# The first block's way out computed transposed, and its window attention by pairs of heads

## The chip, the cores and the metric

One NeuronCore of one Trainium2 chip runs the program. The metric is the device time of one execution in microseconds (us); lower is better. The core's engines work through their own instruction queues: PE (TensorE, matrix products), DVE (VectorE), ACT (ScalarE), POOL (GpSimd) and SP (SyncE, which issues the DMAs).

## The reference

A first block turns `x` (256 tokens, width 1024) into a new `x`; two layers of a second block follow. What the change touches, cut down:

```python
# first block
o_na = window_attention(q, k, v, kc, vc, rpb)        # 8 heads of 64; per head 256 queries
#   s  = concat([q k_band^T + bias (masked by column), q kc^T])   # 256 x 512 per head
#   pr = softmax(s);  o = pr[:, :256] v + pr[:, 256:] vc
o_dn = bidirectional_delta_rule(...)                  # chunks of 64, 8 heads
u_na = (o_na * silu(z_na)) @ w_o_na
u_dn = (rmsnorm(o_dn) * silu(z_dn)) @ w_o_dn
y    = sigmoid(g_na) * u_na + sigmoid(g_dn) * u_dn
x    = x + gate * (y @ w_out)                         # gate: a third of silu(c) @ mod_w + mod_b
# second block, i = 0, 1
x = layer_norm(ALPHA * x + 0.5 * swiglu(x, ffn1_up[i], ffn1_down[i]))
...
ple = sigmoid(x @ w_ple_gate[i]) * (p[i] @ w_ple[i])
...
```

## The kernel before, in words

All weights stream once from HBM. `block` loads a block of up to 128x1024 (`raw<-W`, issued by SP, line 108), ACT rounds it to the high part `wh` (line 119), and DVE or POOL subtracts for the low part `wl` (line 122); the letters of `self.low` choose which of the two. `mm3` (lines 146 to 150) then makes three products, high by high, high by low and low by high. `raw` has three buffers and `wh` and `wl` four each. Products of data that is not split are plain fp32; the trace shows two records for each of those.

The order of instructions on every engine is fixed when the program is built, by a scheduler that simulates a timeline: it starts from program order and pulls later work forward where an engine would be idle and the buffers are there. So the projections `z_na`, `z_dn`, `g_na` and part of `o_na` are traced after the attention, and run between its instructions.

In the first block the order of the code is: modulation and projections; a loop over 8 heads that builds the two triangular matrices of the delta rule (lines 621 to 645); `invert_blocks` (lines 650 to 682), 31 steps of two multiplications and two subtractions on DVE, each on the result of the step before; `attend` for 8 heads (lines 415 to 446); `levels32` and `levels64` on PE, which need the inverse; the steps of the state; the gates, `o_na`, `g_dn` and `o_dn`; the projection `out` (lines 952 to 958).

`attend(h)` works on 2 tiles of 128 queries by 512 keys. Even heads use the PSUM banks of `nab` (two), odd ones those of `st` (four, shared with the loop over the triangular matrices). Per tile: scores on PE (L433: 64 rows of the array, even heads the first 64 and odd heads the last 64), bias and maximum on DVE (L435, L436), exponential with the sum on ACT (L437), reciprocal on DVE (L438), a scaling of all 512 columns on ACT (L439), four transpositions on PE into one bank and a copy on ACT (`rows_T`, L373 and L376), and then eight products with the values (L445), whose output is on partitions 0 to 63 for even heads and 64 to 127 for odd ones. The bias tile (two buffers) is loaded by two DMAs (L422), masked on POOL (L423), and last read by L435.

The way out: `out` is computed with the tokens on the partitions, in four PSUM banks, 512 columns wide: first output columns 0 to 511 for k = 0 to 7, then 512 to 1023. `mod_gate` has made `gate` as rows on all partitions (L902, L904). Two DVE operations for each quarter (L966, L967) make `x1`. `second` then builds the rope tables (L1025 to L1049, on DVE with two sines on ACT), transposes `x1` on PE (16 times, L1068) and splits the result (L153, L154), makes the projection `ple(0)` (24 products of 512 columns), multiplies `x1` by ALPHA on POOL (L999), and starts the feed-forward network `ffn` (L1155): for each f of 22 two `up` products of 24 matmuls of 256 columns, and `down` products.

Of the kernel before, what the change touches and what calls it, by code (L numbers as in the profile page):

```python
# [92 lines left out]
class Kernel:  # L93
# [84 lines left out]
    def run(self):  # L178
        nc = self.nc
        with self.st:  # L180
            one = self.one = self.pool("one")
            self.st_p = self.pool("st", 4, space=PSUM)


            self.cols = one.tile([128, 192], FP32, name="cols")[:, 0:NCOLS]
            self.ident = one.tile([128, 128], FP32, name="ident")
            self.mhalf = self.pool("edge", side="right").tile([128, 24], FP32, name="mhalf")[:, 0:1]
            nc.vector.memset(self.mhalf, -0.5)
            with ExitStack() as s1:
                x1 = self.first(s1)  # L190
                if self.upto == "first":
                    nc.sync.dma_start(out=self.out.rearrange("(t p) d -> p t d", p=128), in_=x1)
                    return
            with ExitStack() as s2:
                self.second(s2, x1)
# [6 lines left out]
    def first(self, st):  # L202
# [15 lines left out]
        P4, PR, MR, S1, X8 = tag("P4", 1024, 1, early), tag("PR", 256, 2, early), tag("MR", 512, 1), tag("S1", 512, 2, early), tag("X8", 2048, 1, self.one)  # L218
# [26 lines left out]
        sel4 = one.tile([4, 2], FP32, name="sel4")  # L245
        nc.vector.tensor_tensor(out=sel4, in0=self.ident[0:4, 0:2], in1=self.ident[0:4, 2:4], op=ALU.add)

        sel3 = one.tile([4, 1], FP32, name="sel3")
        nc.vector.tensor_tensor(out=sel3, in0=sel4[:, 0:1], in1=self.ident[0:4, 1:2], op=ALU.add)
# [70 lines left out]
        identR = one.tile([128, 128], F32R, name="identR")  # L320
# [8 lines left out]
        ones = one.tile([128, 16], FP32, name="ones")[:, 0:1]  # L329
        nc.vector.memset(ones, 1.0)  # L330
        ab = one.tile([128, 32], FP32, name="ab")
# [4 lines left out]
        xT[0] = tuple(one.tile([128, 8, 256], F32R, name=n) for n in ("xh", "xl"))  # L336
# [78 lines left out]
        def attend(h, ways=0):  # L415

            e, j = h % 2, h // 2
            sl = slice(64 * e, 64 * e + 64)
            bank, P = (nab, F2) if ways == 0 else (self.bank, U2)
            bias = one.tile([128, 6, 64], FP32, tag="bias", bufs=2, name="bias")  # L420
            for r2 in range(2):
                nc.sync.dma_start(out=bias[64 * r2:64 * r2 + 64], in_=I["rpb"][:, h, 1 - r2:7 - r2, :])  # L422
            nc.gpsimd.tensor_tensor(out=bias, in0=bias, in1=cc["namask"].unsqueeze(1).to_broadcast([128, 6, 64]), op=ALU.add)  # L423
            if ways == 0:
                pt = P4().rearrange("p (t c q) -> p t c q", t=2, c=4)
                pt = [pt[:, 0], pt[:, 1]]
            else:
                pt = [Y2().rearrange("p (c q) -> p c q", c=4) for _ in range(2)]
            ps, pr = [bank() for _ in range(2)], [P() for _ in range(2)]
            mx = one.tile([128, 4], FP32, tag="smmx", bufs=4, name="mx")  # L430
            mx, rs = mx[:, 0:2], mx[:, 2:4]
            for t in range(2):
                nc.tensor.matmul(out=ps[t], lhsT=nqT[sl, j, t * 128:(t + 1) * 128], rhs=nkT[sl, j, :], start=True, stop=True)  # L433
            for t in range(2):
                nc.vector.tensor_tensor(out=ps[t][:, 0:256], in0=ps[t][:, 0:256], in1=bias[:, 2 - 2 * t:6 - 2 * t, :].rearrange("p e c -> p (e c)"), op=ALU.add)  # L435
                nc.vector.tensor_reduce(out=mx[:, t:t + 1], in_=ps[t], axis=AX.X, op=ALU.max, negate=True)  # L436
                nc.scalar.activation(out=pr[t], in_=ps[t], func=ACT.Exp, bias=mx[:, t:t + 1], accum_out=rs[:, t:t + 1])  # L437
                nc.vector.reciprocal(out=rs[:, t:t + 1], in_=rs[:, t:t + 1])  # L438
                nc.scalar.mul(out=pr[t], in_=pr[t], mul=rs[:, t:t + 1])  # L439
            for t in range(2):  # L440
                rows_T(pr[t], pt[t], 0, bank=bank)
            po = bank()
            for t in range(2):
                for c in range(4):
                    nc.tensor.matmul(out=po[sl, t * 128:(t + 1) * 128], lhsT=nv[:, c, h * 64:(h + 1) * 64], rhs=pt[t][:, c, :], start=(c == 0), stop=(c == 3))  # L445
            nc.scalar.copy(out=oT[sl, j, :], in_=po[sl, 0:256])
# [367 lines left out]
        for h in range(8):  # L814
            attend(h, h % 2)
# [75 lines left out]
        gate = None  # L891

        def mod_gate(c):

            nonlocal gate
# [56 lines left out]
        ps = [[acc() for _ in range(2)], [nab() for _ in range(2)]]  # L952
        for c in range(2):
            for k in range(8):
                w = self.block(("out", k), c, 2)
                for t in range(2):
# [786 lines left out]
```

## Time and profile before

| | us |
|---|---|
| median of 3 runs | 1791.49 |
| lowest, highest | 1790.18, 1792.56 |
| the profiled execution | 1789.8 |
| span of its profile | 1787.9 |
| PE busy in it | 1701.7 |

Times in the rows are in us from the start of the span. A row of the timeline or of the chain has a start and a duration. `PE` is the matrix product and `PEld` the load of its stationary operand, which overlaps it. "x8" means that eight like instructions in a row are merged; in the timeline, the duration of such a row includes the tail of the last one, and in the chain it does not. Matmuls are pipelined, so what one costs is the distance between the starts of two neighbours, which is shorter than its own duration. A bracket at the end of a row is the idle time of that engine before it and what ended it. PEclk is the granted clock of TensorE as a share of full speed: 1.00 is 2.4 GHz, 0.50 is 1.2 GHz.

### The profile page before, as it was taken

To read this page: it belongs to the slowest core of one execution; us is meant where nothing else is said; L and a number is where in the kernel's file an instruction comes from. 1 tells how busy PE (TensorE), PEld (TensorE's weight loads), DVE (VectorE), ACT (ScalarE), POOL (GpSimd) and SP (SyncE) were. 2 spreads that over 40 slices of the span, in tenths; PEclk is the share of its full clock that TensorE was granted. 3 is DMA by queue.
4 is the path that set the end of the run, shared out by engine and by line. 5 is a ranking of instruction groups with operands and counts; after the bars stand their busy time and mean duration, and the time that the engine had idled before them with its cause. 6 is when DMAs were issued, how large, how long until landed. Compare 5 with 4: busy or idle time off the path is not lost.

```text
span 1787.9 us, 30317 instructions
## 1 busy us (share of the span) xinstructions
PE 1701.7 (95%) x12186; PEld 1527.8 (85%) x12186; DVE 1108.0 (62%) x1657; ACT 852.7 (48%) x1372; POOL 350.2 (20%) x235
## 2 busy tenths in 40 slices
PE   6899989999979999999989999899999999989998
PEld 2898866899869998889978999799997899879997
DVE  6774388645665556774676555755568646675556
ACT  6444575433444444653445444444445534444442
POOL 6335342312130002210231000300005103130000
PEclk9899998779989999999999999899999999999999
DMA  7223221312456565544556656565664445645563
GB/s 287 78 83 112 76 67 54 99 41 96 160 199 197 189 201 171 196 149 152 194 166 190 191 191 206 156 205 189 197 204 161 143 164 180 201 162 191 191 208 108
DMA packets 91827, 286.17 MB, mean 160 GB/s; under 512 B 10916, under 2 KB 13476, under 8 KB 91688
## 3 DMA queue, kind: packets, MB, share of 16 engines
q1 hardware_dynamic: 91400, 284.10, 49.1%
q8 instruction: 95, 1.56, 0.4%
q14 instruction: 44, 0.36, 0.1%
q10 hardware_dynamic: 288, 0.16, 0.0%
HBM read 283.17 MB, written 1.05 MB: 159 GB/s over the span
## 4 chain that ended last, share of the span: by engine, by line
PE 79%; DVE 9%; DMA 3%; issue 3%; ACT 2%; POOL 1%; SPq 0%; DVEq 0%; ACTq 0%; POOLq 0%
PE acc L148 13%; PE acc L149 13%; PE acc L150 13%; PE ps L149 10%; PE ps L148 10%; PE ps L150 10%; DMA raw<-W 3%; DVE wl L122 2%; ACT wh L119 1%; PE ps L795 1%; PE ps L725 1%; PE ps L373 1%; DVE PR L671 1%; PE ps L751 1%; PE ps L743 1%
## 5 line engine op out<-in xcount | busy, mean ns | idle before, releaser
L122 DVE TENSOR_TENSOR wl<-raw,wh 128x1024 fp32r<-128x1024 f32 (+1 forms) x462 | 551.0, 1196 | 424.2 <-ACT wh L119 420.9
L119 ACT CAST wh<-raw 128x1024 fp32r<-128x1024 f32 (+1 forms) x535 | 497.8, 934 | 620.8 <-PE acc L149 159.0
L148 PE MATMUL ps<-XH,wh 128*128 128x256 f32 x1408 | 394.9, 281 | 7.1 <-DVE XH L1114 6.7
L149 PE MATMUL ps<-XL,wh 128*128 128x256 f32 x1408 | 395.1, 281 | 5.7 <-DVE XL L154 5.7
L150 PE MATMUL ps<-XH,wl 128*128 128x256 f32 x1408 | 394.0, 280 | 0.0
L148 PEld LDWEIGHTS ps<-XH,wh 128*128 128x128 f32 x1408 | 267.4, 190 | 11.1 <-DVE XH L1114 6.9
L149 PEld LDWEIGHTS ps<-XL,wh 128*128 128x128 f32 x1408 | 266.7, 189 | 9.8 <-DVE XL L154 6.2
L150 PEld LDWEIGHTS ps<-XH,wl 128*128 128x128 f32 x1408 | 268.5, 191 | 0.0
L175 POOL TENSOR_TENSOR rs<-rs,mhalf 128x1 f32<-128x1 f32 x16 | 10.6, 667 | 848.0 <-DVE rs L170 848.0
L122 POOL TENSOR_TENSOR wl<-raw,wh 128x512 fp32r<-128x512 f32 (+1 forms) x73 | 111.1, 1525 | 239.8 <-ACT wh L119 212.2
L148 PE MATMUL acc<-XH,wh 128*128 128x256 f32 x544 | 156.1, 287 | 0.0
L149 PE MATMUL acc<-XL,wh 128*128 128x256 f32 x544 | 153.8, 283 | 0.0
L150 PE MATMUL acc<-XH,wl 128*128 128x256 f32 x544 | 153.7, 283 | 0.0
L148 PEld LDWEIGHTS acc<-XH,wh 128*128 128x128 f32 x544 | 104.7, 192 | 2.0 <-issue 1.0
L150 PEld LDWEIGHTS acc<-XH,wl 128*128 128x128 f32 x544 | 105.1, 193 | 0.0
L149 PEld LDWEIGHTS acc<-XL,wh 128*128 128x128 f32 x544 | 104.4, 192 | 0.0
L148 PE MATMUL acc<-xh,wh 128*128 128x256 f32 (+1 forms) x296 | 88.4, 300 | 8.8 <-ACT wh L119 5.0
L148 PE MATMUL acc<-wh,XH 128*128 128x512 f32 (+1 forms) x216 | 80.0, 405 | 15.5 <-DVE XH L1114 15.2
L150 PE MATMUL acc<-xh,wl 128*128 128x256 f32 (+1 forms) x296 | 88.5, 299 | 3.9 <-DVE wl L122 2.4
L149 PE MATMUL acc<-wl,XH 128*128 128x512 f32 (+1 forms) x216 | 86.8, 403 | 2.6 <-DVE wl L122 2.6
L150 PE MATMUL acc<-wh,H 128*128 128x512 f32 x224 | 88.3, 394 | 0.0
L148 PE MATMUL acc<-wh,H 128*128 128x512 f32 x224 | 88.1, 393 | 0.0
(599 smaller groups left out, 3414.9 us busy)
## 6 DMA issues: line engine op xcount, KB each, us to landing
raw<-W SPq DMA_DIRECT2D x420, 512.0 KB, 4.2
raw<-W SPq DMA_DIRECT2D x145, 256.0 KB, 2.9
GB<-lngb SPq DMA_DIRECT2D x12, 512.0 KB, 5.1
L<-W SPq DMA_DIRECT2D x5, 512.0 KB, 7.4
bias<-rpb SPq DMA_DIRECT2D x16, 96.0 KB, 2.5
M<-c SPq DMA_DIRECT2D x2, 768.0 KB, 4.6
GB<-c SPq DMA_DIRECT2D x2, 768.0 KB, 4.7
A<-x SPq DMA_DIRECT2D x1, 1024.0 KB, 11.1
```

The source lines that it names most:

```text
L119: self.nc.scalar.copy(out=h, in_=raw)
L122: e.tensor_tensor(out=lo, in0=raw, in1=h, op=ALU.subtract)
L148: mm(out=out, lhsT=a[0], rhs=b[0], start=first, stop=False)
L149: mm(out=out, lhsT=a[0], rhs=b[1], start=False, stop=False)
L150: mm(out=out, lhsT=a[1], rhs=b[0], start=False, stop=last)
L175: nc.gpsimd.tensor_tensor(out=out, in0=out, in1=e.to_broadcast(shape), op=ALU.pow)
L373: nc.tensor.transpose(ps[:, j * 128:(j + 1) * 128], src[:, j * 128:(j + 1) * 128], self.ident)
L671: nc.vector.tensor_tensor(out=pr[d], in0=Ln[d][:, j + 1:32, j:j + 1].to_broadcast(sh), in1=X[d][:, j:j + 1, 0:j + 1].to_broadcast(sh), op= ...
L725: nc.tensor.matmul(out=p2[quad[a], m, :], lhsT=tt[quad[b], m, :], rhs=Yd[quad[b], h * 4 + t, :], start=True, stop=True, tile_position=(32 ...
L743: nc.tensor.matmul(out=p1[sb, m, :], lhsT=LTs[d][sa, h, t, sb], rhs=X64[sa, h * 4 + t, :], start=True, stop=True)
L751: nc.tensor.matmul(out=p2[sa, m, :], lhsT=tt[sb, m, :], rhs=LTs[d][sb, h, t, sb], start=True, stop=True)
L795: nc.tensor.matmul(out=pv[:, c], lhsT=LT[:, h, t, :], rhs=r[:, c], start=True, stop=True)
```

## The change

Way out. `out` is computed transposed: the weight block is the stationary operand (blocks are now columns of `w_out`), the output has its 128 output columns on the partitions and 256 tokens across, m = 0 to 7, 24 matmuls of 256 columns each. One DVE operation adds the transposed `x` times the gate, now a column per partition, and a split writes straight into the feed-forward network's input. The 16 transpositions and the four pairs of DVE operations on rows are gone. The rows of `x` times ALPHA, which the first norm needs, are made in `ffn` after f = 4 by 32 products with the identity and four scalings on ACT; the rope tables come after f = 7, and the `ple` projection of layer 0 after f = 10. `mod_gate` transposes its row with eight products of 2 columns, and adds the bias from a constant already there, in place of a DMA and one product of 512 columns.

Attention. `attend(j)` takes heads 2j and 2j+1 together: the score products and the value products of the two alternate. The scaling of the probabilities is gone; the identity is scaled by the reciprocals instead (128 columns, written into the bias tile), and the transposition is a plain product with it. Both heads' values go into one `st` bank, with one copy out.

```diff
+            self.XHa, self.XLa, self.X8 = (tag(n) for n in ("XHa", "XLa", "X8"))
+            self.xt0 = self.new_xt(0)
...
-        def attend(h, ways=0):
...
+        def attend(j):
+            heads = []
+            for e in range(2):
+                h = 2 * j + e
+                bank, P = (nab, F2) if e == 0 else (self.bank, U2)
+                bias = one.tile([128, 6, 64], FP32, tag="bias", bufs=2, name="bias")
...
             for t in range(2):
+                for e, (h, bank, bias, pt, ps, pr, mx, rs) in enumerate(heads):
+                    sl = slice(64 * e, 64 * e + 64)
+                    nc.tensor.matmul(out=ps[t], lhsT=nqT[sl, j, t * 128:(t + 1) * 128], rhs=nkT[sl, j, :], start=True, stop=True)
             for t in range(2):
-                nc.vector.reciprocal(out=rs[:, t:t + 1], in_=rs[:, t:t + 1])
-                nc.scalar.mul(out=pr[t], in_=pr[t], mul=rs[:, t:t + 1])
-            for t in range(2):
-                rows_T(pr[t], pt[t], 0, bank=bank)
-            po = bank()
+                for h, bank, bias, pt, ps, pr, mx, rs in heads:
...
+            for h, bank, bias, pt, ps, pr, mx, rs in heads:
+                nc.vector.reciprocal(out=rs, in_=rs)
+                dg = bias.rearrange("p e c -> p (e c)")
+                for t in range(2):
+                    nc.scalar.mul(out=dg[:, t * 128:(t + 1) * 128], in_=self.ident, mul=rs[:, t:t + 1])
+                for t in range(2):
+                    pp = bank()
+                    for c in range(4):
+                        nc.tensor.matmul(out=pp[:, c * 128:(c + 1) * 128], lhsT=pr[t][:, c * 128:(c + 1) * 128], rhs=dg[:, t * 128:(t + 1) * 128],
+                                         start=True, stop=True)
+                    nc.scalar.copy(out=pt[t], in_=pp.rearrange("p (c q) -> p c q", c=4))
+            po = self.bank()
             for t in range(2):
                 for c in range(4):
+                    for e, (h, bank, bias, pt, ps, pr, mx, rs) in enumerate(heads):
+                        nc.tensor.matmul(out=po[64 * e:64 * e + 64, t * 128:(t + 1) * 128], lhsT=nv[:, c, h * 64:(h + 1) * 64], rhs=pt[t][:, c, :],
+                                         start=(c == 0), stop=(c == 3))
+            nc.scalar.copy(out=oT[:, j, :], in_=po[:, 0:256])
...
         def mod_gate(c):
...
-            nc.sync.dma_start(out=r[1:2, :], in_=I["mod_bg"][:, c * 512:(c + 1) * 512])
             ps = nab()
-            nc.tensor.matmul(out=ps, lhsT=sel3.to_broadcast([4, 128]), rhs=r, start=True, stop=True)
-            gate = gate if c else N4()
-            nc.scalar.mul(out=gate[:, c * 512:(c + 1) * 512], in_=ps, mul=0.5)
+            for q in range(4):
+                nc.tensor.matmul(out=ps[:, 2 * q:2 * q + 2], lhsT=r[:, q * 128:(q + 1) * 128], rhs=sel4, start=True, stop=True)
+            g = gcol[:, c * 4:c * 4 + 4]
...
-        ps = [[acc() for _ in range(2)], [nab() for _ in range(2)]]
-        for c in range(2):
...
+        x0 = Q8().rearrange("p (k t) -> p k t", k=8)
+        nc.sync.dma_start(out=x0, in_=I["xT"])
+        xt = self.new_xt(0)
+        for m in range(8):
+            w = self.blockv(("out", m), "p (k c) -> p k c", k=8)
+            ps = (acc if m % 2 else nab)()[:, 0:256]
             for k in range(8):
+                self.mm3(ps, (w[0][:, k, :], w[1][:, k, :]), (yh[:, k, :], yl[:, k, :]), k == 0, k == 7)
+            v = T2()[:, 0:256]
+            nc.vector.scalar_tensor_tensor(out=v, in0=ps, scalar=gcol[:, m:m + 1], in1=x0[:, m, :], op0=ALU.mult, op1=ALU.add)
+            self.split(xt[0][:, m, :], xt[1][:, m, :], v)
+        return xt
...
-        self.rope_tables()
-        xt = self.transposed(x1)
+        xa = self.X8().rearrange("p (t d) -> p t d", t=2)
+        def first_rows():
+            for t in range(2):
+                for c in range(2):
+                    ps = self.bank()
+                    for k in range(4):
+                        for a in range(2):
+                            nc.tensor.matmul(out=ps[:, k * 128:(k + 1) * 128], lhsT=xt[a][:, 4 * c + k, t * 128:(t + 1) * 128], rhs=self.identR, start=a == 0, stop=a == 1)
+                    nc.scalar.mul(out=xa[:, t, c * 512:(c + 1) * 512], in_=ps, mul=ALPHA)
...
-        nc.gpsimd.tensor_scalar(out=xa, in0=xa, scalar1=ALPHA, scalar2=None, op0=ALU.mult)
         for i in range(2):
-            xt = self.norm(self.ffn(1, i, xt), 0.5, xa, i, 0)
+            xt = self.norm(self.ffn(1, i, xt, {4: first_rows, 7: self.rope_tables, 10: first_ple} if i == 0 else {}), 0.5, xa, i, 0)
...
-    for k in range(8):
-        put(("out", k), inp["w_out"][0][k * 128:(k + 1) * 128])
+    for m in range(8):
+        put(("out", m), kpc(inp["w_out"][0][:, m * 128:(m + 1) * 128], 8))
```

`first_ple` calls `ple_rows`, which makes the same 24 products as `ple` in `st` banks, two at a time. In the second block `XH` and `XL` have one buffer each beside `XHa` and `XLa`, in place of two each.

## Rows read from the trace of the kernel before

**Rows 1.** The page, busy time of the engines over the span.
```profile
PE 1701.7 (95%) x12186; PEld 1527.8 (85%) x12186; DVE 1108.0 (62%) x1657; ACT 852.7 (48%) x1372; POOL 350.2 (20%) x235
```
**Rows 2.** Stretches of 20 us: PE, PEld, DVE, ACT, POOL busy (x); PEclk, DMA, GB/s.
```profile
500.00:520.00 20.00, 9.77 (x41) 8.07 (x40) 17.15 (x24) 8.19 (x12) 15.56 (x5) 0.68 0.53 175
540.00:560.00 20.00, 20.00 (x142) 18.58 (x141) 10.26 (x13) 9.27 (x14) 0.00 (x0) 1.00 0.62 193
```
**Rows 3.** Timeline, 495 to 522: PE, DVE and POOL at the way out.
```profile
495.20 1.03 PE L1068 MATMUL ps<-ident,X 128*128 128x128 f32 x8
...
500.89 0.40 PE L150 MATMUL nab<-wh,B 128*128 128x512 f32 x1
502.07 3.88 DVE L967 TENSOR_TENSOR X<-X,L 128x512 f32<-128x512 f32 x2
503.24 0.66 PE L1068 MATMUL ps<-ident,X 128*128 128x128 f32 x4 [1.96 <-DVE X L967]
506.00 1.11 PE L1068 MATMUL ps<-ident,X 128*128 128x128 f32 x4 [2.10 <-DVE X L967]
508.13 5.37 POOL L999 TENSOR_SCALAR X<-X 128x2048 f32<-128x2048 f32 x1
509.25 4.28 DVE L1031 CAST pf<-pos 128x2 f32<-128x2 int32 x1 [0.71 <-DMA pos<-pos]
510.52 0.41 PE L148 MATMUL ps<-XH,wh 128*128 128x256 f32 x1
515.94 0.68 DVE L154 TENSOR_TENSOR XL<-ps,XH 128x512 fp32r<-128x512 f32 x1
516.67 0.58 PE L149 MATMUL ps<-XL,wh 128*128 128x256 f32 x1 [5.74 <-DVE XL L154]
...
521.20 0.40 PE L148 MATMUL acc<-wh,M 128*128 128x512 f32 x1
```
**Rows 4.** Timeline, two neighbouring matmuls of 256 columns at full clock.
```profile
238.02 0.28 PE L150 MATMUL acc<-xh,wl 128*128 128x256 f32 x1
238.14 0.29 PE L148 MATMUL acc<-xh,wh 128*128 128x256 f32 x1
```
**Rows 5.** Pieces of the chain that ended last: start, us, what, records.
```profile
31.31 1.05 PE ps L303 x8
...
188.56 0.87 PE ps L373 x8
...
197.71 1.91 PE nab L433 x4
...
213.14 1.02 PE nab L445 x8
...
412.26 0.89 PE ps L789 x8
...
419.45 1.05 PE nab L902 x2
...
794.46 1.01 PE ps L1482 x8
```
**Rows 6.** Timeline of PE: value products of an even (nab) and an odd head alternating.
```profile
297.62 0.27 PE L445 MATMUL nab<-P,NV 128*64 128x128 f32 x1
297.67 0.27 PE L445 MATMUL ps<-Y,NV 128*64 128x128 f32 x1
297.73 0.27 PE L445 MATMUL nab<-P,NV 128*64 128x128 f32 x1
```
**Rows 7.** A stretch of 5 us in the attention; columns as in the 20 us stretches.
```profile
270.00:275.00 5.00, 5.00 (x11) 2.13 (x10) 2.41 (x8) 0.80 (x3) 0.99 (x1) 0.50 0.00 0
```
**Rows 8.** Timeline of DVE: the last step of the inversion.
```profile
333.71 1.99 DVE L680 STREAM_TRANSPOSE L<-L 128x1024 f32<-128x1024 f32 x1
```
**Rows 9.** Timeline of SP's queue: DMA issues around the late heads.
```profile
263.98 11.87 SPq L422 DMA_DIRECT2D bias<-rpb  x6
293.58 47.39 SPq L108 DMA_DIRECT2D raw<-W  x22
```

More of the change, by code (lines that the diff above doesn't have):

```diff
@@ L319, in first @@
             cc[n] = c1[:, a:a + C1[n][1]]
-        identR = one.tile([128, 128], F32R, name="identR")
+        identR = self.identR
         nc.vector.tensor_copy(out=identR, in_=self.ident)
@@ L335, in first @@
         xT = {}
-        xT[0] = tuple(one.tile([128, 8, 256], F32R, name=n) for n in ("xh", "xl"))
+        xT[0] = self.xt0
         xc = B16(F32R).rearrange("p (a k t) -> p a k t", a=2, k=8)
@@ L413, in first @@
         oT = one.tile([128, 4, 256], FP32, name="oT")
-        def attend(h, ways=0):
[L417 to L431, printed above, removed]
+        def attend(j):
[4 more added lines that the diff above has]
+                bias = one.tile([128, 6, 64], FP32, tag="bias", bufs=2, name="bias")
+                for r2 in range(2):
+                    nc.sync.dma_start(out=bias[64 * r2:64 * r2 + 64], in_=I["rpb"][:, h, 1 - r2:7 - r2, :])
+                nc.gpsimd.tensor_tensor(out=bias, in0=bias, in1=cc["namask"].unsqueeze(1).to_broadcast([128, 6, 64]), op=ALU.add)
+                if e == 0:
+                    pt = P4().rearrange("p (t c q) -> p t c q", t=2, c=4)
+                    pt = [pt[:, 0], pt[:, 1]]
+                else:
+                    pt = [Y2().rearrange("p (c q) -> p c q", c=4) for _ in range(2)]
+                mx = one.tile([128, 4], FP32, tag="smmx", bufs=4, name="mx")
+                heads.append((h, bank, bias, pt, [bank() for _ in range(2)], [P() for _ in range(2)], mx[:, 0:2], mx[:, 2:4]))
@@ L813, in first @@
         XY = invert_blocks()
-        for h in range(8):
-            attend(h, h % 2)
+        for j in range(4):
+            attend(j)
         def go(*gens):
@@ L1153, in rows_acc, with ffn @@
         return {(t, c): self.acc1() for t in range(2) for c in range(2)}
-    def ffn(self, j, i, xt):
+    def ffn(self, j, i, xt, between={}):
         nc = self.nc
@@ L1187, in ffn @@
                 down(f - 2)
+            if f in between:
+                between[f]()
         down(NF - 2)
@@ L1208, in ple, with ple_rows @@
         yield out
+    def ple_rows(self, i):
+        nc = self.nc
+        p = self.U2().rearrange("p (k t) -> p k t", k=2)
+        nc.sync.dma_start(out=p, in_=self.i["pT"][i])
+        ph = self.M6(F32R)[:, 0:1024].rearrange("p (a k t) -> p a k t", a=2, k=2)
+        self.split(ph[:, 0], ph[:, 1], p)
+        w = [self.block(("ple", i, k)) for k in range(2)]
+        out = self.PL8().rearrange("p (t d) -> p t d", t=2)
+        for t in range(2):
+            acc = {(t, c): self.bank() for c in range(2)}
+            for k in range(2):
+                self.down(acc, w[k], (ph[:, 0, k, :], ph[:, 1, k, :]), k == 0, k == 1, (t,))
+            for c in range(2):
+                nc.scalar.copy(out=out[:, t, c * 512:(c + 1) * 512], in_=acc[t, c])
+        return out
     def ple_gate(self, i, xt, xa, plr):
```

92 lines of the change are left out of this document (32 added, 60 removed).

## The prediction

> **What bounds the kernel now.** I read the page first: PE is busy 95% of the span [rows 1]. So time goes away where PE does not work, works at the low clock, or does work that can be dropped. The table of stretches shows where the first two are. From 540 on PE has no gap at clock 1.00 while the DMAs are 62% busy [rows 2], and the stretches that follow look the same; there a product more or less shows in full. The worst stretch of the whole span is 500 to 520, the way out of the first block: PE 9.77 of 20 us, clock 0.68 [rows 2]. The timeline of that place gives the reasons in order [rows 3]. The last product of `out` starts at 500.89. PE then waits 1.96 and 2.10 us for L967 on DVE, whose two operations take 3.88 us, and starts on `up`. After 510.52 it stands for 5.74 us: the fourth split (L154) sits on DVE behind the rope tables' first cast, L1031, which took 4.28 us for two columns and ended with L999, the multiplication by ALPHA that POOL ran from 508.13 to 513.50. At 521.20 PE is back at its pace.
>
> For the attention I read the chain and the timeline of PE, DVE and SP. Around 270 PE has only the attention: 11 matmul records in 5 us at clock 0.50 [rows 7]. The inversion on DVE ends at 335.7 [rows 8], and `levels32` can't start earlier. Between these two, PE's time is partly spare.
>
> **Way out: what goes.** From 500.89 plus its slot of 0.24 (twice the 0.12 between neighbours of 256 columns [rows 4]) to 521.20 are 20.1 us. Useful work at full clock in it: 24 matmuls of `up`, 24 x 0.12 = 2.9, and four of `ple`, 4 x 0.24 = 1.0. The other 16.2 are waits, the low clock and eight transpositions. Eight more at 495.20 [rows 3] cost 0.9 (8 in 0.87 [rows 5]). Together -17.1.
>
> **What comes in its place.** `out` itself stays equal: 96 matmuls of 512 columns become 192 of 256, the same 192 x 0.12. After the last m, `up` needs that block's result only at its k = 7, 21 x 0.12 = 2.5 us later; three operations half as wide as the 0.68 of L154 [rows 3] are then done, even at 3 x 0.68 = 2.0. At the start, m = 0 wants all of `y` at once, where the old order wanted it over eight long steps; the last part of `o_dn` takes four operations, 4 x 0.68 = 2.7, against 18 x 0.12 = 2.2 of m = 0 that don't need it, and as much of m = 1. I take +1 for both ends; without the cover it is 3. The 32 products with the identity run where PE has no gap. The trace shows no product of 128 columns in the split form: half of a 256 column slot would be 0.06, a plain fp32 product 0.22 (two records of L789, 8 in 0.89 [rows 5]). I take 0.11, the transposition's price [rows 5], since that also streams 128 columns through a fresh 128x128 operand: 32 x 0.11 = +3.5, between 1.9 and 7.1. The 24 `ple` products only move. The rope tables and the four scalings move under `ffn`, where DVE is busy 10.26 and ACT 9.27 of 20 us [rows 2], and a `down` follows its f by two; without that cover a stall like the 5.74 us [rows 3] would come back. POOL loses L999, so DVE's cast has nothing to wait for. On SP one load of 1 MB replaces two of half that, two small loads go, and `pos`, `freq` and `pT` are issued behind the first `up` weights, off the path. Sum of the way out: -17.1 + 1 + 3.5 = **-12.6**, between -15.2 and -7.0.
>
> **The gate.** Two products of 512 columns (two records, 1.05 us each at the full clock) become eight small ones, 16 records at 0.13 (8 in 1.05), 2.1 us both [rows 5]: **0**, within 1.
>
> **Attention.** PE's work for 8 heads at the full clock, from [rows 5]: scores 32 records x 0.48 = 15.3; values 128 x 0.128 = 16.3; transpositions 64 x 0.109 = 7.0; together 38.6. After: a transposition that scales is a plain product, two records at 0.11, 128 x 0.11 = 14.2. For the values the trace of before already shows what alternation does: where an even and an odd head happened to run together, starts came 0.05 to 0.06 apart instead of 0.128 [rows 6], so 128 x 0.055 = 7.0. For the scores (64 rows of the array each) no pair is shown. The nearest row is L1482, where the halves of rows and of columns alternate: 8 records of 256 columns in 1.01, 0.126 each [rows 5], against 0.24 for half of a 512 column score record. At that ratio the scores take 8.1. Sum 29.3, that is -9.3; if nothing overlaps, 15.3 + 16.3 + 14.2 = 45.8, that is +7.2.
>
> The Trainium skill, TensorE: Matmul & The Clock Gate, under Terms, says of PE's transposition mode that it is four times as fast for fp32 as a product, which speaks against this edit. Here the records give 0.22 against 0.109, twice. By the page the sum would be 64 x (0.44 - 0.22) = 13.7 us worse.
>
> How much of this reaches the end? Little of PE's time around 270 is asked for by anything else, and the inversion ends at 335.7 whatever PE does. Freed time pays only as far as later projections move into it. ACT loses the 512 wide scalings, which helps the chain of each head. On the other side, the bias tile is now held until the transposing products of its pair are done, so SP's next bias loads wait longer, and weight loads queue behind them. And odd heads still can't start before the loop over the triangular matrices lets go of `st`, and now the even one's values wait for them. I take **-4**, a little under half of the -9.3, and keep -9.3 to +7.2 for the range.
>
> **Sum.** -12.6 + 0 - 4 = -16.6 on the profiled execution of 1789.8 us (span 1787.9 and 1.9 around it), 1773.2; the median of the runs is 1.7 above it, 1774.9. So 1775, with a range of its own of 1766 to 1784.
>
> **Rivals.** (a) Pairing gives all it can. The -9.3 arrive whole, and the 5 us at the low clock [rows 7] fill up with projections: -12.6 - 9.3 - 5 = -26.9, 1765. For it: that stretch is nearly empty. Against: weights have to be there for the fill, and SP issued none from 275.85 to 293.58 [rows 9].
>
> (b) The pairs don't overlap as said: the scheduler puts other work between the two heads' products, or score products on the two row halves run one after the other. Then the +7.2 stand: -12.6 + 7.2 = -5.4, 1786. For it: the scheduler broke up most pairs that could have met before. Against: they now follow each other in program order.
>
> (c) Slower, by one mechanism: the held bias tile. Six bias issues took SP from 263.98 to 275.85, and the next weight left it at 293.58 [rows 9]. If handing the bias tile from pair to pair makes one more gap like that of 17.7 us, and PE loses all of it, then -12.6 + 17.7 = +5.1, 1797. It decides from 12.6 + 3.6 = 16.2 us of lost fill. For it: tile and queue are both in order. Against: PE's spare time there covers part of such a gap, and it must be lost whole.
>
> (d) The weight stream becomes the limit at the way out. The stall let buffers fill at 175 GB/s; without it the stream must hold the 193 GB/s of the network [rows 2]. Half of the three waits, 9.8 us [rows 3], would come back: 1780. Against: the network runs at that rate without a gap at a DMA share of 0.62.
>
> (e) The product that transposes costs four transpositions: -16.6 + 13.7 = -2.9, 1789. Against it stands L789 [rows 5], a product of that very shape.
>
> **How the numbers follow.** Forecast 0.45, (a) 0.18, (b) 0.17, (c) 0.10, (d) 0.06, (e) 0.04. A measurement of this kernel tells 0.2%, 3.6 us, from no change. Under 1787.9 lie the forecast, (a), (d) and most of (b): 0.83. Between 1787.9 and 1795.1 lie the rest of (b) and (e): 0.07. Above it (c): 0.10. The range from 1762 to 1788 leaves out (c), (e) and the tails of (a) and (b). Most of the chance is on one side, as the way out rests on waits that are in the rows, and its bounds don't reach zero.
>
> **What would show it.** In the profile after: no gap of PE over 1 us between `out` and f = 1, and a clock of 1.00 there; L1031 short; the 32 identity products with starts some 0.11 apart and no wait before f = 5's products. In the attention: value records 0.055 apart and score records 0.25 apart; the transposing products 0.11 per record. `levels32` starting within some 5 us of where it did. It is wrong if `levels32` or the first `out` product moves by over 10 us, if SP shows bias loads that hold back weights for longer than before, or if the stall at the way out only moves to f = 4, 7 or 10.

## The result, and the profile after

The changed kernel takes 1803.29 us (median of 7 executions, 1797.55 to 1808.88) where the kernel before takes 1791.49 (7 executions, 1790.18 to 1793.29). The ratio is 1.0071, with an interval of 1.0055 to 1.0087. It is slower by some 12 us (11.8 between the medians, 12.7 by the ratio); the forecast was 1775 us, and its range ended at 1788. Medians and ratios here leave out an execution at a clearly lower clock; there was one, of e8 (1898.28 us at a mean clock of 0.829). The profiled execution took 1797.55 us (span 1795.7), the quickest of the seven; it is 7.8 us above the profiled execution of before (1789.8).

The page shows PE busy for 10.7 us longer, in 188 more records [rows 1]:

```profile
PE   1712.4 (95%) x12374; PEld 1547.9 (86%) x12374; DVE 1103.9 (61%) x1650; ACT 845.5 (47%) x1365; POOL 338.3 (19%) x232
```

The way out looks as forecast. First the two stretches that answer to [rows 2], then the timeline of PE that answers to [rows 3]: the last product of `out`, the first of `up`, the one wait, and the first two and the last product with the identity.

```profile
500.00:520.00 20.00, 19.74 (x170) 19.54 (x169) 12.93 (x17) 9.54 (x14) 4.45 (x2) 1.00 0.72 235
540.00:560.00 20.00, 20.00 (x152) 19.06 (x151) 8.20 (x11) 9.64 (x14) 0.00 (x0) 1.00 0.49 152
```
```profile
503.84 0.28 PE L150 MATMUL acc<-B,wl 128*128 128x256 f32 x1
503.96 0.28 PE L148 MATMUL ps<-XHa,wh 128*128 128x256 f32 x1
...
506.65 0.38 PE L149 MATMUL ps<-XLa,wh 128*128 128x256 f32 x1 [0.26 <-DVE XLa L154]
...
540.98 0.22 PE L1013 MATMUL ps<-identR,XHa 128*128 128x128 f32 x1
541.04 0.27 PE L1013 MATMUL ps<-identR,XLa 128*128 128x128 f32 x1
...
544.39 0.27 PE L1013 MATMUL ps<-identR,XLa 128*128 128x128 f32 x1
```

`up` follows `out` 0.12 us later, the only wait behind it is 0.26 us, the clock is 1.00, and the 32 identity products take 3.5 us (540.98 to the last start at 544.39 and its slot), 0.11 each. The 16 us of stall are gone.

In the attention the value products overlap as forecast, and the score products do not. The timeline of PE shows sixteen records of transposing products in 1.95 us, and value products of an even and an odd head that start within 0.01 us of each other, pairs 0.11 apart. The score products (L440) of the even heads (nab) and of the odd ones (ps) stand in groups of their own, with other work between them, and never alternate: two records take 1.12 us and four 1.98. PE later stands for 7.19 us, waiting for ACT's scaled identity (the tile `bias`):

```profile
256.47 1.95 PE L454 MATMUL ps<-bias,U 128*128 128x128 f32 x16
...
258.71 1.12 PE L440 MATMUL ps<-X,N 64*128 64x512 f32 x2
...
260.34 0.27 PE L461 MATMUL ps<-Y,NV 128*64 128x128 f32 x1
260.35 0.27 PE L461 MATMUL ps<-P,NV 128*64 128x128 f32 x1
260.45 0.27 PE L461 MATMUL ps<-Y,NV 128*64 128x128 f32 x1
260.46 0.27 PE L461 MATMUL ps<-P,NV 128*64 128x128 f32 x1
...
261.20 1.12 PE L440 MATMUL ps<-X,N 64*128 64x512 f32 x2
...
263.82 1.98 PE L440 MATMUL nab<-X,N 64*128 64x512 f32 x4 [0.47 <-ACT P L456]
...
272.99 3.48 PE L454 MATMUL ps<-bias,U 128*128 128x128 f32 x16 [7.19 <-ACT bias L450]
```

On SP's queue the bias loads of the late heads now hold the place from 259.55 on, and the next weight leaves at 299.89, where it left at 293.58 before [rows 9]:

```profile
259.55 31.44 SPq L428 DMA_DIRECT2D bias<-rpb  x10
299.89 42.52 SPq L108 DMA_DIRECT2D raw<-W  x19
```

Where the time goes is read from a few places along the two timelines, in us from the start:

| place | before | after | difference |
|---|---|---|---|
| first product of `levels32` | 327.8 | 319.8 | -8.0 |
| end of the inversion's last step on DVE | 335.7 | 328.4 | -7.3 |
| last product of the delta rule | 440.8 | 429.8 | -11.0 |
| last projection of 256 columns ahead of `o_dn` | 467.2 | 470.2 | +3.0 |
| end of the last `out` product | 501.3 | 504.1 | +2.8 |
| first norm of the second block, first cast | 708.6 | 701.8 | -6.8 |
| end of the span | 1787.9 | 1795.7 | +7.8 |

Two things are to be seen. Between 430 and 470 us the lead of the delta rule is lost. And behind the first norm, where no line of the code was meant to change, another 14.6 us are lost. In the FFNs there, once they have begun, PE has no gap in either kernel, and its clock is 1.00; what differs is the pace. The rows are of PE, from the second FFN of the second layer: the first product of an `up` group of 48 products, and the first `down` product right behind it.

The kernel before, two groups:
```profile
1616.52 0.28 PE L148 MATMUL ps<-XH,wh 128*128 128x256 f32 x1
1622.17 0.39 PE L148 MATMUL acc<-wh,H 128*128 128x512 f32 x1
1624.95 0.28 PE L148 MATMUL ps<-XH,wh 128*128 128x256 f32 x1
1630.40 0.39 PE L148 MATMUL acc<-wh,H 128*128 128x512 f32 x1
```
The changed kernel, two groups:
```profile
1622.19 0.28 PE L148 MATMUL ps<-XH,wh 128*128 128x256 f32 x1
1627.84 0.40 PE L148 MATMUL acc<-wh,H 128*128 128x512 f32 x1
1630.60 0.28 PE L148 MATMUL ps<-XH,wh 128*128 128x256 f32 x1
1636.26 0.40 PE L148 MATMUL acc<-wh,H 128*128 128x512 f32 x1
```

Before, the groups alternate: 5.65 us (0.1177 a product) and 5.45 us (0.1135). After, each takes 5.65 or 5.66 us. That is 4224 products in the four FFNs, at means of 0.1153 and 0.1178, 10.6 us; and 2016 between the two FFNs of each layer, most of them gate projections, at 0.1157 and 0.1177, 4.0 us: 14.6 together in the second block. The means are over the starts of neighbouring products in the trace. The first of the four FFNs lies ahead of the first norm, so 2.6 of these 14.6 us do, and only 12.0 of the 14.6 lost behind the norm are pace. Most of the rest, 1.6 us in each layer, is in nine products of 512 columns that run at half clock in this execution and at the full clock in the profile of before. Before, then after, in the first layer:

```profile
738.20:742.20 4.00, 4.00 (x18) 3.34 (x19) 4.00 (x10) 1.66 (x3) 0.40 (x1) 1.00 0.43 134
```
```profile
729.40:733.40 4.00, 3.67 (x9) 2.89 (x10) 4.00 (x10) 1.90 (x6) 0.83 (x1) 0.57 0.55 196
```

The stretch of 40 us of gates in each layer shows the same as a count of products, with PE busy throughout; the kernel before had one layer of either pace, the changed kernel two of the slow one. Before, then after:

```profile
840.00:880.00 40.00, 40.00 (x355) 40.00 (x355) 25.54 (x23) 18.12 (x21) 11.99 (x7) 1.00 0.60 196
1480.00:1520.00 40.00, 40.00 (x342) 40.00 (x341) 25.20 (x23) 17.17 (x19) 14.05 (x8) 1.00 0.57 180
```
```profile
840.00:880.00 40.00, 40.00 (x342) 40.00 (x341) 25.19 (x22) 17.62 (x20) 14.08 (x8) 1.00 0.57 186
1480.00:1520.00 40.00, 40.00 (x342) 40.00 (x341) 24.21 (x23) 17.75 (x21) 11.05 (x7) 1.00 0.57 185
```

### The profile page after: what moved, and what is told of

Its sections match the earlier page's. It is cut to its first block, busy times and chain, and to the rows that moved or that the text cites. A ratio compares the mean times of both kernels' runs of the same rounds, so it can differ in the third digit from the quotient of the medians.

```text
span 1795.7 us, 30667 instructions
## 1 busy us (share of the span) xinstructions
PE 1712.4 (95%) x12374; PEld 1547.9 (86%) x12374; DVE 1103.9 (61%) x1650; ACT 845.5 (47%) x1365; POOL 338.3 (19%) x232
## 4 chain that ended last, share of the span: by engine, by line
PE 80%; DVE 7%; DMA 3%; issue 3%; ACT 3%; POOL 2%; DVEq 0%; SPq 0%; ACTq 0%; POOLq 0%
PE acc L148 13%; PE acc L150 13%; PE acc L149 13%; PE ps L148 10%; PE ps L150 10%; PE ps L149 10%; DMA raw<-W 3%; DVE wl L122 2%; ACT wh L119 1%; PE ps L812 1%; PE ps L377 1%; PE ps L734 1%; PE ps L742 1%; PE ps L768 1%; PE ps L760 1%
## 5 line engine op out<-in xcount | busy, mean ns | idle before, releaser
L148 PE MATMUL ps<-XHa,wh 128*128 128x256 f32 x704 | 197.5, 281 | 6.8 <-DVE XHa L1123 6.8
L149 PE MATMUL ps<-XLa,wh 128*128 128x256 f32 x704 | 197.2, 280 | 0.3 <-DVE XLa L154 0.3
L150 PE MATMUL ps<-XHa,wl 128*128 128x256 f32 x704 | 197.0, 280 | 0.0
L148 PE MATMUL ps<-XH,wh 128*128 128x256 f32 x704 | 196.9, 280 | 0.0
L150 PE MATMUL ps<-XH,wl 128*128 128x256 f32 x704 | 196.7, 279 | 0.0
L149 PE MATMUL ps<-XL,wh 128*128 128x256 f32 x704 | 196.5, 279 | 0.0
L175 POOL TENSOR_TENSOR rs<-rs,mhalf 128x1 f32<-128x1 f32 x16 | 10.6, 665 | 860.6 <-DVE rs L170 860.6
L148 PEld LDWEIGHTS ps<-XH,wh 128*128 128x128 f32 x704 | 132.0, 188 | 1.6
L149 PEld LDWEIGHTS ps<-XL,wh 128*128 128x128 f32 x704 | 131.9, 187 | 1.6
L150 PEld LDWEIGHTS ps<-XHa,wl 128*128 128x128 f32 x704 | 132.8, 189 | 0.0
L150 PEld LDWEIGHTS ps<-XH,wl 128*128 128x128 f32 x704 | 132.3, 188 | 0.0
```

Source lines behind the costliest of these rows:

```text
L148: mm(out=out, lhsT=a[0], rhs=b[0], start=first, stop=False)
L149: mm(out=out, lhsT=a[0], rhs=b[1], start=False, stop=False)
L150: mm(out=out, lhsT=a[1], rhs=b[0], start=False, stop=last)
L175: nc.gpsimd.tensor_tensor(out=out, in0=out, in1=e.to_broadcast(shape), op=ALU.pow)
```

## The experiments

**What sets the pace.** The diff changes no product of the second block's FFNs, but it moves tiles. By the layout of the tiles in SBUF, the streamed operand (XH, XL) and the weights (wh, wl) of these products lie 192 bytes apart modulo 256 per partition before (XH at 36416, wh at 200576), and 64 apart after (XHa at 18368, wh at 200576). I call this the distance. The rivals are the place of a group in TensorE's instruction stream, and chance. Two kernels came first. e3 moves the activations only:

```diff
-            self.cols = one.tile([128, 208], FP32, name="cols")[:, 0:NCOLS]
+            self.cols = one.tile([128, 192], FP32, name="cols")[:, 0:NCOLS]
```


> The changed kernel with one tile 64 bytes shorter per partition, so that the activation tiles of the second block lie 64 bytes lower against the weights; the instructions are the same. Theory address: the pace of the FFN products depends on how the activations lie against the weights, so at least one of the four FFNs leaves 0.118 us from start to start. Theory stream (the pace depends on where a group of products begins in TensorE's instruction stream): all four FFNs keep 0.118 us, and the time lies between 1797 and 1809 us.

All four FFNs left 0.118 us, for 0.120 (5.76 us a group), and one execution took 1810.81 us. In the gates, too:

```profile
1633.90 0.28 PE L148 MATMUL ps<-XH,wh 128*128 128x256 f32 x1
1639.66 0.39 PE L148 MATMUL acc<-wh,H 128*128 128x512 f32 x1
```
```profile
840.00:880.00 40.00, 40.00 (x336) 40.00 (x335) 23.61 (x22) 17.18 (x19) 12.18 (x8) 1.00 0.57 184
```

e4 leaves the tiles and moves the instructions (the extra products' results are not used):

```diff
     def ffn(self, j, i, xt, between={}):
+        for _ in range({(1, 0): 1, (2, 0): 1, (1, 1): 2, (2, 1): 4}[j, i]):
+            ps = self.bank()
+            nc.tensor.matmul(out=ps[:, 0:128], lhsT=self.identR, rhs=self.identR, start=True, stop=True)
```


> The changed kernel with one, one, two and four small extra products of 128 columns (0.1 us each) ahead of the four FFNs, so that the instructions behind them stand 1, 2, 4 and 8 products later in TensorE's stream. Theory stream: in at least one of the four FFNs groups of products leave 0.118 us for 0.1135 us or less, and the time falls by about 3.5 us (950 products x 0.0043 us) or more for each FFN that does. Theory address or chance: all four keep 0.118 us and the time lies between 1797 and 1810 us.

Three FFNs kept 0.118 throughout. In the first one nearly all of the 144 products ahead of the first `down` ran at 0.1133, 0.6 us in all, and the rest at 0.118. The time of its one execution, 1793.53 us, lies below what the address gives, so e4 by itself leaves both open.

The control is the kernel before with nothing but one tile 128 bytes wider, which puts the second block at the distance of the changed kernel:

```diff
-            self.cols = one.tile([128, 192], FP32, name="cols")[:, 0:NCOLS]
+            self.cols = one.tile([128, 224], FP32, name="cols")[:, 0:NCOLS]
```


> The kernel before, with one small tile 128 bytes wider per partition and nothing else: every instruction stays, but the activations of the second block lie against the weights as in the changed kernel (64 bytes apart modulo 256, where the kernel before has 192). Theory address: all products of 256 columns in the second block stand 0.118 us apart instead of 0.115 on the mean, 6300 x 0.0025 = 15 us more, 1804 us where the kernel before takes 1789. Rival (the pace comes from the order of the work in the changed kernel): alternating 0.1135 and 0.118 us as before, and 1789 us within 4.

It took 1804.02 us against 1789.75, ratio 1.0085 (1.0065 to 1.0105). Every FFN group and both layers of gates stand at 0.118, and the first block is as long as before (last `out` product at 501.3 in both profiles). So a kernel that does not change one instruction loses 14.3 us, about what the pace costs the changed kernel.

The other way round, e6 is the whole change with the weights of the second block 128 bytes lower, which restores 192 (`ab` gives up padding and `sg` shares the tile of `cT` to make room):

```diff
-            self.ones = self.pool("edge", side="right").tile([128, 24], FP32, name="ones")[:, 0:1]
+            self.ones = self.pool("edge", side="right").tile([128, 56], FP32, name="ones")[:, 0:1]
```


> The whole change, with the weight tiles of the second block 128 bytes lower, so that activations and weights lie 192 bytes apart modulo 256 as in the kernel before (two small tiles share room to make place for it). Theory address: the products of 256 columns fall back to the mean of before, 0.1155 us, and the time falls by 15 us, to 1786 us where the kernel before takes 1789. Rival: 0.118 us and about 1801 us.

1782.34 us against 1789.75, ratio 0.9967 (0.9945 to 0.9989): the change now gains. The groups alternate again:

```profile
1606.15 0.28 PE L148 MATMUL ps<-XH,wh 128*128 128x256 f32 x1
1611.81 0.39 PE L148 MATMUL acc<-wh,H 128*128 128x512 f32 x1
1614.58 0.28 PE L148 MATMUL ps<-XH,wh 128*128 128x256 f32 x1
1620.03 0.39 PE L148 MATMUL acc<-wh,H 128*128 128x512 f32 x1
```

**The two halves.** e1 is the changed kernel with the attention of before:

```diff
-        for j in range(4):
-            attend(j)
+        for h in range(8):
+            attend(h, h % 2)
```


> Only the way out (out products transposed, gate as a column, first block handed over without the row form, the identity products moved behind f = 4); attention is that of the kernel before. Theory 1, attention is what costs the first block its time: the first norm of the second block comes about 12 us earlier than before, near 696 us. Rival, the way out itself costs it: the first norm stays near 702 us or later. The whole time then goes by the pace of the 256-column products of the FFNs: near 1779 us if they keep the mean of before (0.115 to 0.117 us from start to start), near 1792 us if all of them stand 0.118 us apart as in the changed kernel.

1796.55 us against 1788.61, ratio 1.0045 (1.0028 to 1.0063). The first norm came at 704.9, of which 2.6 us are the slow pace of one FFN (1056 x 0.0025): that is the rival's "702 us or later", though 3.7 us earlier than before. e7 is the same with the weights moved as in e6:

> The way out alone (attention as before), with the weights placed as in the run before this one, 192 bytes apart modulo 256. Theory address: 15 us less than the way out alone at 64 bytes, 1781.5 us where the kernel before takes 1789, the best so far. Rival (the way out gains nothing, and the pace is not the address's): 1790 us or more.

1783.81 us against 1789.75, ratio 0.9976 (0.9959 to 0.9994). So the way out by itself gains about 6 us, half of what I had summed. e2 is the kernel before with the new attention:

```diff
-        for h in range(8):
-            attend(h, h % 2)
+        for j in range(4):
+            attend(j)
```


> Only the attention by pairs; the way out is that of the kernel before. Theory 1: the delta rule ends some 8 us earlier, but the weights that the fill lacks in attention are paid between 430 and 480 us, and the first norm comes about 5 us later than before, near 714 us. Rival: the pairs by themselves gain, and the first norm comes at or before 705 us. Whole time: near 1796 us with the pace of the FFN products as before, near 1809 us with 0.118 us throughout; the rival about 1786 us.

1793.63 us, ratio 1.0024 (1.0008 to 1.0041): the attention costs some 4 us where I had -4. Its first norm came at 711.0, 2.4 later than before. e8 tried the distance that was missing, with the way out alone (`edge` 40 columns wide):

> The way out alone, with the weights 64 bytes lower: 128 bytes apart modulo 256, a distance that no run here has shown yet (0: 0.120 us; 64: 0.118; 192: 0.1135 and 0.118 alternating). Theory address: the pace is some other constant. If 128 is the farthest from a clash, all groups stand 0.1135 us apart or less, and the time is 10 us or more below that at 192 bytes, near 1770 us; if the pace goes by the parity of 128 bytes alone, 0.120 us and 1808 us.

0.1187 us on the mean throughout, 1809.80 us (three executions) against 1789.75, ratio 1.0109 (1.0082 to 1.0137). 128 is neither the best distance, nor as bad as 0:

```profile
840.00:880.00 40.00, 40.00 (x339) 40.00 (x338) 23.82 (x22) 17.18 (x19) 12.16 (x8) 1.00 0.56 184
```

**Two paces at one distance.** At 192 a group has one of two paces. e9 asked whether the instruction stream decides, with four more products (not used) ahead of the second block of e7:

```diff
+        ps = self.bank()
+        for _ in range(4):
+            nc.tensor.matmul(out=ps[:, 0:128], lhsT=self.identR, rhs=self.identR, start=True, stop=True)
         self.low = "p"
         for i in range(2):
```


> The way out alone at 192 bytes (1783.8 us), with four small products (8 instructions of TensorE, 0.4 us) ahead of the second block. At 192 bytes groups of products run at one of two paces, 0.1135 or 0.118 us, and in this kernel the 1008 products of 256 columns of the gates stand at 0.118 in both layers. Theory stream (which of the two it is goes by the place of the group in the instruction stream, modulo 16 instructions): all groups change sides, FFN groups alternate the other way round, the gates of both layers go to 0.1135, 2 x 1008 x 0.0044 = 9 us less, near 1775 us. Rival (chance, or something older in the pipeline): the gates stay at 0.118 in at least one layer, and the time stays within 1779 to 1788 us.

The gates did change to 0.114 in both layers, but the first FFN's groups kept their sides, and the time didn't follow: 1784.11 us, ratio 0.9974 (0.9957 to 0.9991), as e7. So I ran e7's very program again:

> The way out alone at 192 bytes once more, for a second profile of the same program. Theory stream (the program fixes which of the two paces a group has): the gates of both layers stand 0.118 us apart again. Rival (chance, from one execution to the next): at least one layer's gates stand at 0.1135.

The gates of e7, first execution, then second:

```profile
840.00:880.00 40.00, 40.00 (x342) 40.00 (x341) 25.23 (x23) 17.17 (x19) 13.98 (x8) 1.00 0.55 183
1480.00:1520.00 40.00, 40.00 (x342) 40.00 (x341) 25.15 (x22) 17.60 (x20) 14.04 (x8) 1.00 0.55 185
```
```profile
840.00:880.00 40.00, 40.00 (x356) 40.00 (x355) 25.52 (x24) 18.66 (x21) 14.13 (x8) 1.00 0.57 185
1480.00:1520.00 40.00, 40.00 (x356) 40.00 (x355) 24.30 (x22) 18.55 (x21) 12.30 (x7) 1.00 0.58 189
```

One program, and both layers of gates changed sides. The stream theory falls: it is the single execution. The two spans are 1788.0 and 1782.6 us, 5.4 apart, and 4.6 of that lies behind the first norm. A profile of one execution at this distance is therefore known only to some 5 us. What picks the pace stays open. At distance 64 the changed kernel's first 20 products of `up` ran at 0.1133, until the wait of 0.26 us at 506.65 above; behind it they ran at 0.118. In e4, which had no wait there, some 140 did. So the distance decides which pace the products mostly have, and it isn't the only thing that does.

**The attention's loss.** The prediction's rival (c) says that the held bias tile keeps weights off SP. e10 gives the scaled identity a tile of its own, and the bias tile comes free after the addition, as before:

```diff
-                dg = bias.rearrange("p e c -> p (e c)")
+                dg = T2()
```


> Attention alone as changed, but the scaled identity has a tile of its own, so that the bias tile comes free after the addition, as before. Theory held tile: the 5 us that the attention alone costs go away, 1789 us where the kernel before takes 1789.5, and the bias loads of the late heads stop SP for less time. Rival (the pairs themselves cost it: what waits for two heads waits longer): 1793 to 1795 us, as the attention alone.

1786.52 us against 1790.08, ratio 0.9985 (0.9968 to 1.0003): the loss is gone, and it may be a small gain. SP gets back to the weights 10 us earlier than in e2, and PE does 61 more records between 265 and 300 us. `levels32` starts at 328.4, as before (327.8); its early start, 320.6 in e2 and 319.8 in the changed kernel, went away with the loss. The rows are of e2, then of e10 (SP's queue, then the stretch):

```profile
262.57 28.27 SPq L424 DMA_DIRECT2D bias<-rpb  x10
300.74 40.57 SPq L108 DMA_DIRECT2D raw<-W  x19
```
```profile
265.00:300.00 35.00, 28.35 (x195) 19.79 (x191) 32.34 (x91) 18.21 (x45) 7.52 (x5) 0.90 0.09 24
```
```profile
269.20 5.49 SPq L424 DMA_DIRECT2D bias<-rpb  x4
290.50 51.16 SPq L108 DMA_DIRECT2D raw<-W  x23
```
```profile
265.00:300.00 35.00, 33.68 (x256) 25.86 (x254) 32.49 (x79) 20.37 (x48) 12.12 (x7) 0.95 0.14 43
```

e11 keeps the pairs and divides as before; e12 keeps single heads and divides in the transposing product, with the scaled identity in the bias tile:

```diff
                 nc.vector.reciprocal(out=rs, in_=rs)
+                for t in range(2):
+                    nc.scalar.mul(out=pr[t], in_=pr[t], mul=rs[:, t:t + 1])
+                for t in range(2):
+                    rows_T(pr[t], pt[t], 0, bank=bank)
```


> Pairs of heads, but the division as before (ScalarE scales the rows, then plain transpositions). Theory pairs: the cost is theirs, 1794 us or more where the kernel before takes 1789.5, and TensorE has the same idle stretch between 265 and 300 us. Rival (the transposing product costs it): within 3 us of the kernel before.

```diff
             for t in range(2):
-                rows_T(pr[t], pt[t], 0, bank=bank)
+                pp = bank()
+                for c in range(4):
+                    nc.tensor.matmul(out=pp[:, c * 128:(c + 1) * 128], lhsT=pr[t][:, c * 128:(c + 1) * 128], rhs=dg[:, t * 128:(t + 1) * 128],
+                                     start=True, stop=True)
```


> One head after the other as before, but the division in the transposing product, with the scaled identity in the bias tile. Theory pairs: within 3 us of the kernel before, 1789.5, or a little below, as ScalarE's work in each head gets shorter. Rival (the transposing product and the held tile cost it): 1794 us or more.

e11 took 1799.90 us, ratio 1.0068 (1.0043 to 1.0092), e12 1792.82 us, ratio 1.0024 (1.0003 to 1.0045). So either edit alone costs time, pairs without the shorter division most; of these kernels only e10, with both edits and the bias tile free, loses nothing. Single heads with the shorter division and a tile of its own were not run, so e12's loss may be that of the held tile. In the profiled executions the weights came back on SP at 290.5 (e10), 293.6 (before), 300.7 (e2), 301.5 (e11) and 306.9 us (e12), and the last `out` product ended in the same order: 498.9, 501.3, 502.6, 510.6, 512.6. The medians have another order (e12's profile is of its slowest execution, 1800.41 us, and e11's of its fastest, 1794.15), so this order says little of sizes. The longest time that SP issues no weight around there is 22.5 us in e10, 31.0 before, 38.0 in e11, 40.1 in e2 and 42.3 in e12: longer than before in all three that lose. For e10 against e2 the cause is shown, since the edit is the tile alone (the order that the scheduler gives SP and PE changes with it); for e11, which holds no tile, it stays open what delays the weights.

**The way out's missing half.** In e7 the last `out` product ended at 510.3, in e15 at 509.5, against 501.3 before. The groups of DMA issues between 380 and 480 us show what was moved there; the kernel before, then e7:

```profile
raw<-W SPq DMA_DIRECT2D x39, 256.0 KB, 3.1
L<-x SPq DMA_DIRECT2D x2, 512.0 KB, 7.3
```
```profile
raw<-W SPq DMA_DIRECT2D x32, 256.0 KB, 3.1
raw<-W SPq DMA_DIRECT2D x7, 512.0 KB, 4.9
Q<-xT SPq DMA_DIRECT2D x1, 1024.0 KB, 8.4
```

Seven `out` loads and the input go out among the last projections' weights, and the seven are now twice as large: 4.5 MB in place of 2.75. e13 is e7 with halves again:

```diff
-            w = self.blockv(("out", m), "p (k c) -> p k c", k=8)
             ps = (acc if m % 2 else nab)()[:, 0:256]
-            for k in range(8):
-                self.mm3(ps, (w[0][:, k, :], w[1][:, k, :]), (yh[:, k, :], yl[:, k, :]), k == 0, k == 7)
+            for k, w in self.halves(("out", m), 8):
+                self.mm3(ps, w, (yh[:, k, :], yl[:, k, :]), k == 0, k == 7)
```


> The way out alone at 192 bytes, with the weights of the out products loaded in halves of 256 KB, as the kernel before does, in place of whole blocks of 512 KB; the products stay. Theory weight loads (seven of these loads and the input stand on SP's queue among the last weights of the projections; whole blocks put 4.5 MB there in place of 2.75, about 6 us at 300 GB/s): the last out product ends near 503 us in place of 509 to 510, and the time falls by about 6 us, to 1778 us where the kernel before takes 1790. Rival (the projections are late for another reason): 1782 to 1786 us, and the last out product still ends at 508 us or later.

The last `out` product ended at 507.0, about 3 us earlier, and not at 503. The time did not fall: 1783.84 us against 1790.01, ratio 0.9967 (0.9948 to 0.9987), and the first norm came at 706.0 (705.6 and 704.8 in the two executions of e7). What the halves gave ahead of `up` was lost again behind it, where PE now waits 1.9 us for POOL's `wl`. The theory of the doubled loads falls as the cause of the whole. Even the 3 us are uncertain: the changed kernel and e3, whose products come in the same order, end the last `out` product at 504.1 and 508.0. e14 puts the three mends together on the full change:

> Both halves of the change with all three mends: weights 192 bytes from the activations, the scaled identity in a tile of its own, the out weights in halves. Theory (the three losses are separate): about 1773 to 1777 us where the kernel before takes 1790, as the prediction had it for the whole change. Rival (the gains of attention and way out don't add, since the same projections wait for weights in both): 1780 us or more.

1779.23 us against 1790.01, ratio 0.9937 (0.9919 to 0.9956): the fastest kernel here, between the two expectations. Its last `out` product ended at 500.2 and its first norm came at 699.1.

## Why the prediction was wrong, point by point

**What failed is a term that wasn't in the sum.** The diff's tile edits (`cols` 208 wide, XH and XL single, XHa and XLa in `one`) were costed nowhere, and the reading of [rows 2], that from 540 us on "a product more or less shows in full", took the price of a product itself as fixed at the 0.12 of [rows 4]. e5 shows that the layout alone costs 14.3 us, where the whole forecast gain was 16.6, and e6 beside the changed kernel that it turned a gain of 0.33% into a loss of 0.71%. No rival had it. In the profile this term is 2.6 us ahead of the first norm and 12.0 behind it. The Trainium skill, SBUF — State Buffer, under "SBUF: two separate sides", says that contention happens only on the port that GpSimd and VectorE share and at the DMA's ports; by that, where TensorE's operands lie would cost nothing. Here e5 measures 14.3 us, so the measurement decides.

**Way out: the mechanism right, half of its gain lost ahead of it.** From the end of the last `out` product to the first norm the changed kernel took 197.7 us where before took 207.3: -9.6, and -12.3 with the 2.6 us of pace taken out, against -12.6 forecast; at the distance of before it took 195.3 in e6, e7 and e15, -12.0. The identity products cost 3.5 us, as forecast, the start of `up` 0.12 and 0.26 us (+1 forecast), and the stall did not move to f = 4, 7 or 10. But the way out alone gained 6 us in its median, as the last `out` product came later than before in each profile of the way out alone. The step "`out` itself stays equal" looked at its products alone; its loads doubled in size and stand among the projections' weights. e13 shows that this explains at most 3 of the 6 to 9 us, and that mending it doesn't pay. What the rest is stays open; the outcome is like rival (d), whose 5 us are the right size, but not in the place it named.

**Attention: two of PE's three prices right, the sign wrong.** The value products (0.055 a record) and the transposing products (0.11 at the full clock) came as summed, and the factor of four that the Trainium skill states (TensorE: Matmul & The Clock Gate, under Terms; rival e) does not show here: 16 records in 1.95 us. The score products did not: summed at 0.25 a record, 8.1 us, they keep 0.43 to 0.53, since the scheduler put other work between the two heads' score products, as rival (b) had it. With the 15.3 of before for them PE's sum is 36.5 against 38.6, -2.1 in place of -9.3. Nor was `levels32` bound to 335.7, as the reading of [rows 8] has it: its first product is at 327.8 in the very kernel before, and the last step of the inversion, which was to end at 335.7 "whatever PE does", ends at 328.4 after. So `levels32` started 8 us earlier, and yet the result is +0.24% (e2). The step that gave the wrong sign is the weighing at the end of that part: the held bias tile was named, given a chance of 0.10, and set off against "PE's spare time". It was the larger part: e10, without it, loses nothing. SP was without weights from 259.5 to 299.9, 40 us in place of 31, and the fill that PE did not get then it had to do behind the delta rule, between 430 and 450 us. Before, then after:

```profile
430.00:450.00 20.00, 20.00 (x176) 19.98 (x175) 10.27 (x17) 9.23 (x17) 6.90 (x5) 1.00 0.38 127
```
```profile
430.00:450.00 20.00, 16.61 (x99) 15.11 (x98) 16.03 (x20) 11.10 (x17) 7.95 (x5) 0.74 0.78 270
```

PE is short of 3.4 us and runs at a clock of 0.74 while the DMAs work at 0.78: the lead of 11 us is spent on waiting for weights. Rival (c) had the mechanism; its price, 17.7 us, was too high, and it needed no 16.2 us of lost fill to be felt, since the other terms were smaller too. (In rival (e), 64 x 0.22 is 14.1 and not 13.7, which changes nothing.)

**The gate** came as forecast, within what can be seen. **The sum, mended:** with the layout of before, a tile for the scaled identity and the loads in halves the change takes 0.63% off, 1779 us, inside the forecast's own range of 1766 to 1784. What isn't settled: why the changed kernel's median is 5.7 us above its profiled execution, as its gates have one pace only; the rest of the way out's late start; and what picks between the two paces.

## What to carry to other kernels

An edit that adds, widens or drops a tile moves others, so compare for the products that fill the time how the streamed operand lies against the weights before and after, and run the old kernel with that shift alone before you credit or blame the edit. A tile that gets a second job is held longer: look for the load that waits for it, and for what is queued behind that load. When a stage gets shorter, ask which loads its next stage needs and when their queue issued them.

## What the runs showed of the hardware

Start to start, products of 256 columns in the split form at a granted clock of 1.00, by the distance of streamed operand and weights modulo 256 bytes:

| distance | pace, us | shown by |
|---|---|---|
| 0 | 0.120 | e3 |
| 64 | 0.118, but 0.1133 for some 20 to 140 products behind `out` | after, e1, e4; e5 0.118 only |
| 128 | 0.1187 | e8 |
| 192 | 0.1135 or 0.118 | before, e2, e6, e7, e9 to e15 |

The two paces at 192 alternate from f to f within an FFN (but for its last five f), hold through the gate projections of a layer, and differ between two executions of one program. 64 and 192 were each had with two different placements (before and e6; after and e5), so it is the distance and not the place. Distances between these steps of 64 bytes were not tried.
